# A hybrid trunk's S5 outputs with inputs and states as the stationary operand, and their way back to channels by TensorE

## The chip, the cores and the metric

The kernel runs on one core of a Trainium2 chip. The metric is the device time of one execution in microseconds (us). Five engines work beside each other, each through its own instructions in order: TensorE (PE), VectorE (DVE), ScalarE (ACT), GpSimd (POOL) and SyncE (SP), which issues most DMA transfers.

## The reference, cut to what matters

A trunk of two layers works on 512 tokens, 256 of context and 256 latent, of 1024 channels. In each layer four token mixers of 256 channels each (gated linear attention, retention, S5 and a gated delta rule) stand beside each other, and then a mixture of experts follows. The change touches the S5 mixer alone: a complex diagonal state-space model in both directions in 16 groups of 16 channels with 64 states, then a gelu and a gate.

```python
    ug = uf.reshape(B_, T, S5_GROUPS, S5_GROUP_CH)
    bu = lax.complex(jnp.einsum('gpc,btgc->btgp', b_re.astype(F32), ug),
                     jnp.einsum('gpc,btgc->btgp', b_im.astype(F32), ug))
...
    h = _bidirectional(run_f, run_b, ctx_f, lat_f, ctx_b, lat_b, h0)
    cmat = lax.complex(c_re.astype(F32), c_im.astype(F32))
    y = jnp.real(jnp.einsum('gcp,btgp->btgc', cmat, h)).reshape(B_, T, MIX_W) + d_skip.astype(F32) * uf
    y = jax.nn.gelu(y)
    return y * jax.nn.sigmoid(y @ glu_w.astype(F32) + glu_b.astype(F32))
```

## The kernel before

Activations stand with channels on the 128 partitions and tokens along the free dimension. In `mixers()` a layer projects its normed input to all heads (`project()`, L1387), weight block by weight block: every product is three fp32r products (`product3`, of a high and a low part of the weights and of the input). These are by far the most of TensorE's instructions in this part of the program. Blocks of the conditioning products (`ps_mods`, L1300 and L1305) lie between them. Beside the projections run the delta rule `dn()` and S5 `s5()`. Later come the GLA, retention, the output projection and the experts.

S5 works on chunks of 8 tokens. A chunk's input of a group is a column of 128 values (8 steps by 16 channels), and there are 64 chunks. In layer 1 only the last 32 are needed for the output (c0 = 32; nch is 64 in layer 0 and 32 in layer 1). For each half of the groups (8 groups at a time) it makes matrices (`ps_s_kk`, then s_T through DRAM scratch, s_E, s_inj), brings the inputs into states (`ps_s_I`, L1107), copies them (s_I, L1110), combines and scans them (L1115 to L1127) into the chunk states s_W (L1130 to L1133), and makes the outputs: the matrix Tm (s_T) times the inputs u plus the matrices E times the states W, into one PSUM bank `ps_s_y` (L1142, L1144). Tm and E are stationary and the chunks move, so the outputs stand with (step, channel of a group) on the partitions and (group, chunk) along the free dimension. ScalarE copies them out (L1146). A gelu by s_z follows (L1148 to L1155). The gate wants channels on the partitions. So SP writes s_y to a DRAM scratch (L1156) and 16 DMAs bring it back as s_yt (L1164). The gate is the product `ps_s_glu` (L1171), a sigmoid and a multiplication (s_out, L1177), which the output projection reads as mix_hi.

The delta rule prepares its chunk matrices on VectorE: dn_kt (L661) and dn_x (L688) from TensorE's `ps_dn` products (L654, L685), a blocked inversion in dn_G, dn_X and dn_P (L474 to L497), a round trip of dn_G through DRAM to dn_bd (L704, L724), then the products with dn_bd and dn_x (L743) and the recursion over chunks (L776, L786 and later).

The order of the instructions on each engine is not the order of the code. A scheduler with a simulated timeline chooses among the ready instructions by priorities that the code gives (`k.order(...)` with a small table for each layer), within the PSUM banks and buffers of two tracks. S5's first part, its outputs and its gate are three steps of one generator, with priorities of their own.

Of the kernel before, what the change touches and what calls it, by code (L numbers as in the profile page):

```python
# [6 lines left out]
F32 = mybir.dt.float32  # L7
# [3 lines left out]
AF = mybir.ActivationFunctionType  # L11
ALU = mybir.AluOpType
# [967 lines left out]
def s5(k, dram, dramk, st, get, bc, dskip, gw, gb, t0):  # L980
# [3 lines left out]


    nc, C = k.nc, k.C
    v, e = nc.vector, nc.gpsimd
    lr, li, bsr, bsi, r8, c8, s8 = st
    c0 = 32 * (t0 // 2)
    nch = 64 - c0  # L990
    f, b = slice(0, 64), slice(64, 128)
# [91 lines left out]
    for n in (1, 2, 4, 8, 16, 32):  # L1083
        m = min(n, 63 - n)
# [5 lines left out]
    su = get()  # L1090
    d0 = dram[0].rearrange("(s c) (h g n) -> h s g c n", s=8, h=2, g=8)
    for h in range(2):
        for s in range(8):
            nc.sync.dma_start(d0[h, s], su[:, h, s])
    u = k.u("s5_u")
    nc.sync.dma_start(u, dram[0])
    u = u.rearrange("p (g n) -> p g n", g=16)
    y = None
    for h in range(2):
# [36 lines left out]
        if y is None:  # L1136
            y = k.u("s5_y", 16 * nch).rearrange("p (g n) -> p g n", g=16)
        p = k.bank("s5_y")
        pv = p[:, :8 * nch].rearrange("p (g n) -> p g n", g=8)
        for g in range(8):  # L1140
            gg = 8 * h + g
            nc.tensor.matmul(pv[:, g], Tm[:, g], u[:, gg, c0:], start=True, stop=False)  # L1142
            for i in range(2):
                nc.tensor.matmul(pv[:, g], E[i][:, g].rearrange("p t c -> p (t c)"), W[i][:, gg, c0:], start=False,  # L1144
                                 stop=i == 1)
        nc.scalar.activation(y[:, hs], pv, AF.Copy)  # L1146
    z = k.u("s5_z", 16 * nch).rearrange("p (g n) -> p g n", g=16)
    nc.scalar.activation(z, y, AF.Square)  # L1148
# [5 lines left out]
    sigmoid(nc, z)  # L1154
    e.tensor_tensor(y, y, z, ALU.mult)  # L1155
    nc.sync.dma_start(dram[1][:, :16 * nch], y)  # L1156
    yield
    k.track = "b"

    d1 = dram[1][:, :16 * nch].rearrange("(s c) (h g n) -> h s g c n", s=8, h=2, g=8)  # L1160
    yt = k.u("s5_yt", 16 * nch).rearrange("p (h s n) -> p h s n", h=2, s=8)
    for h in range(2):
        for s in range(8):
            nc.sync.dma_start(yt[:, h, s], d1[h, s])  # L1164
    gw = gw()
# [41 lines left out]


def small_params(a):


    def per_part(x):

        x = np.asarray(x)
        return np.moveaxis(x.reshape(-1, 128), 1, 0)
# [20 lines left out]
    for i in range(2):  # L1236
# [5 lines left out]
        blocks[f"skip{i}"] = d.reshape(128, 64)  # L1242
        blocks[f"glu_b{i}"] = per_part(np.asarray(a["s5_glu_b"])[i])
        dl = np.asarray(a["ret_decay_logit"])[i]
# [12 lines left out]
def arrays(a):  # L1257
# [9 lines left out]
    for j, load in enumerate(LOADS):  # L1267
        cols = np.concatenate([w[..., SECTIONS[n][0]:SECTIONS[n][1]] for n in load], -1)
        out[f"w_in{j}"] = cols.transpose(0, 2, 1, 3).reshape(2, 128, -1)
    out["w_out"] = a["w_out"].reshape(2, 8, 128, 4, 256).transpose(0, 3, 2, 1, 4).reshape(8, 128, 2048)  # L1270

# [9 lines left out]
    bc = []  # L1281
# [4 lines left out]
    out["s5_bc"] = np.stack(bc, 2).reshape(2, 128, 1024)  # L1286
    out["glu_w"] = a["s5_glu_w"].reshape(2, 2, 128, 256).transpose(0, 2, 1, 3).reshape(2, 128, 512)
    return {n: np.ascontiguousarray(x, dtype=np.float32) for n, x in out.items()}
# [154 lines left out]
def mixers(k, I, P, S, modulated, load_w, between, layer, bc):  # L1443
# [73 lines left out]
    if bc is None:  # L1517
        bc = k.u("s5_bc")
        nc.sync.dma_start(bc, I["s5_bc"][layer])
    m_s5 = s5(k, S["dram"][2:4], S["dram5"], S["s5"][layer], s5_in, bc.rearrange("p (a n) -> p a n", a=4),  # L1520
              P[f"skip{layer}"].rearrange("p (s c) -> p s c", s=4), glu_w, P[f"glu_b{layer}"], t0)
# [600 lines left out]
def trunk(tc, I, out):  # L2122
    nc = tc.nc
    from contextlib import ExitStack
    with ExitStack() as st:
# [20 lines left out]
        def rows(src):  # L2146
            x = Rows(k, "xT", T, "b")
            for i, t in enumerate(x.t):
# [6 lines left out]
        mod = [pp.tile([128, 48, 2], F32, name=f"mod{i}") for i in range(2)]  # L2155
        S = dict(dram=[dr.tile([128, 1024], F32, name=f"scratch{i}") for i in range(4)],
                 dram5=[dr.tile([16, 8, 240], F32, name=f"scratch5{i}") for i in range(2)],
# [111 lines left out]
```

## Time and profile before

| | us |
|---|---|
| median of 3 runs | 1472.41 (1470.89 to 1476.87) |
| the profiled execution | 1470.13 |
| its span, first to last instruction | 1468.2 |
| TensorE busy | 1304.2 |
| VectorE busy | 786.3 |
| ScalarE busy | 467.1 |
| mean granted clock of TensorE | 0.937 |

Layer 0's mixers with their output projection run to about 470 us, and its experts follow. The projections of layer 1 begin at 847, its output projection ends at about 1180, and its experts end the program. The profile is of one execution. Times in its rows count from the first instruction.

### The profile page before, as it was taken

To read this page: it belongs to the slowest core of one execution; us is meant where nothing else is said; L and a number is where in the kernel's file an instruction comes from. 1 tells how busy PE (TensorE), PEld (TensorE's weight loads), DVE (VectorE), ACT (ScalarE), POOL (GpSimd) and SP (SyncE) were. 2 spreads that over 40 slices of the span, in tenths; PEclk is the share of its full clock that TensorE was granted. 3 is DMA by queue.
4 is the path that set the end of the run, shared out by engine and by line. 5 is a ranking of instruction groups with operands and counts; after the bars stand their busy time and mean duration, and the time that the engine had idled before them with its cause. 6 is when DMAs were issued, how large, how long until landed. Compare 5 with 4: busy or idle time off the path is not lost. (4 is left out here: it accounts for less than half of the span.)

```text
span 1468.2 us, 28484 instructions
## 1 busy us (share of the span) xinstructions
PE 1304.2 (89%) x11874; PEld 960.7 (65%) x11874; DVE 786.3 (54%) x1560; ACT 467.1 (32%) x778; POOL 187.6 (13%) x265
## 2 busy tenths in 40 slices
PE   4899789999989799999897698968999969999996
PEld 2696569788765577667654396747877746555553
DVE  7799593557453645425524979496467640111112
ACT  4435213434343244323423524312434421000001
POOL 0004112346110000000002100111344100000000
PEclk8999878999999789999999897977999979999999
DMA  9333253245434459999999421254445736999994
GB/s 377 119 108 104 48 187 114 99 156 191 160 123 182 168 206 379 393 373 392 379 391 362 155 82 58 61 187 139 163 158 211 274 141 255 416 415 416 414 413 165
DMA packets 90783, 335.31 MB, mean 228 GB/s; under 512 B 33190, under 2 KB 38120, under 8 KB 62104
## 3 DMA queue, kind: packets, MB, share of 16 engines
q1 hardware_dynamic: 86696, 320.37, 57.6%
q0 software_dynamic: 1648, 7.54, 1.4%
q10 hardware_dynamic: 2304, 5.51, 1.0%
q8 instruction: 97, 1.59, 0.4%
q14 instruction: 38, 0.31, 0.1%
HBM read 312.96 MB, written 20.41 MB: 227 GB/s over the span
## 5 line engine op out<-in xcount | busy, mean ns | idle before, releaser
L1906 PE MATMUL ps_up<-w_moe,xe 128*64 128x256 f32 x1664 | 202.7, 386 | 2.0 <-PEq L1782 2.0
L1906 PEld LDWEIGHTS ps_up<-w_moe,xe 128*64 128x64 f32 x1664 | 122.0, 138 | 73.0 <-issue 20.2
L1387 PE MATMUL ps_project<-h_hi,wi_lo 128*128 128x256 f32 (+1 forms) x568 | 136.1, 306 | 13.0 <-DVE wi_lo L155 13.0
L1387 PE MATMUL ps_project<-h_hi,wi_hi 128*128 128x256 f32 (+1 forms) x568 | 136.8, 308 | 7.6 <-ACT h_hi L1375 4.0
L1387 PE MATMUL ps_project<-h_lo,wi_hi 128*128 128x256 f32 (+1 forms) x568 | 132.4, 300 | 0.3 <-DVE h_lo L1376 0.3
L1387 PEld LDWEIGHTS ps_project<-h_hi,wi_lo 128*128 128x128 f32 (+1 forms) x568 | 97.9, 203 | 20.9 <-DVE wi_lo L155 14.0
L1387 PEld LDWEIGHTS ps_project<-h_hi,wi_hi 128*128 128x128 f32 (+1 forms) x568 | 97.8, 203 | 12.1 <-ACT h_hi L1375 4.1
L1945 PE MATMUL ps_down<-w_moe,actT 128*64 128x512 f32 x416 | 98.2, 597 | 2.7 <-ACT actT L1929 2.7
L155 DVE TENSOR_TENSOR w_moe_lo<-w_moe,w_moe_hi 128x1024 fp32r<-128x1024 f32 x72 | 85.1, 1218 | 28.5 <-ACT w_moe_hi L154 28.5
L1387 PEld LDWEIGHTS ps_project<-h_lo,wi_hi 128*128 128x128 f32 (+1 forms) x568 | 97.3, 202 | 3.1 <-issue 0.9
L154 ACT ACTIVATE w_moe_hi<-w_moe 128x1024 fp32r<-128x1024 f32 x72 | 73.0, 1053 | 28.5 <-DMA w_moe<-in_w_moe 21.6
L1946 DVE COPY y<-ps_down 128x512 f32<-128x512 f32 x26 | 18.0, 691 | 109.4 <-PE ps_down L1945 109.4
L155 DVE TENSOR_TENSOR wi_lo<-ring,wi_hi 128x1024 fp32r<-128x1024 f32 (+1 forms) x50 | 61.0, 1222 | 23.9 <-ACT wi_hi L154 20.8
L154 ACT ACTIVATE wi_hi<-ring 128x1024 fp32r<-128x1024 f32 (+1 forms) x50 | 51.5, 1032 | 66.1 <-PE ps_project L1387 42.4
L1945 PEld LDWEIGHTS ps_down<-w_moe,actT 128*64 128x64 f32 x416 | 29.5, 137 | 51.5 <-issue 45.4
L1929 ACT ACTIVATE actT<-ps_actT 128x256 f32<-128x256 f32 x26 | 10.0, 383 | 154.0 <-PE ps_actT L1926 151.4
L1923 DVE TENSOR_TENSOR act<-act,ps_up 128x256 f32<-128x256 f32 (+1 forms) x32 | 14.9, 466 | 78.2 <-ACT act L1922 67.4
L1300 PE MATMUL ps_mods<-ring,sc 128*32 128x512 f32 x368 | 51.9, 649 | 3.5 <-DVE mod L1307 3.5
L1870 PE MATMUL ps_gather<-sel,h_hi 128*128 128x256 f32 (+1 forms) x256 | 49.6, 310 | 6.0 <-DVE sel L1977 4.0
L2143 POOL DMA_DIRECT2D ring<-in_w_in x4 | 2.5, 612 | 401.5 <-PE ps_up L1906 373.2
L1970 DVE COPY backT<-ps_back 128x256 f32<-128x256 f32 (+1 forms) x17 | 7.5, 439 | 86.4 <-PE ps_back L1968 81.5
L1870 PE MATMUL ps_gather<-sel,h_lo 128*128 128x256 f32 (+1 forms) x256 | 47.8, 303 | 0.0
(559 smaller groups left out, 2793.4 us busy)
## 6 DMA issues: line engine op xcount, KB each, us to landing
w_moe<-in_w_moe SPq DMA_DIRECT2D x144, 1024.0 KB
w_moe<-in_w_moe SPq DMA_DIRECT2D x96, 512.0 KB
ring<-in_w_ada SPq DMA_DIRECT2D x46, 1024.0 KB
ring<-in_w_in SPq DMA_DIRECT2D x21, 1024.0 KB
ring<-in_w_out SPq DMA_DIRECT2D x8, 1024.0 KB
xT<-in_xT SPq DMA_DIRECT2D x8, 512.0 KB
Y<-y ACTq DMA_DIRECT2D x6, 512.0 KB
ring<-in_w_in POOLq DMA_DIRECT2D x3, 1024.0 KB, 7.8
```

The lines of the kernel that those rows point to most:

```text
L154: self.nc.scalar.activation(out[0], src, AF.Copy)
L155: self.nc.vector.tensor_tensor(out[1], src, out[0].bitcast(F32), ALU.subtract)
L1300: nc.tensor.matmul(p[32 * j:32 * j + 32], sc[:, 4 * r + j], w[r][j], start=r == 0, stop=r == 1)
L1387: nc.tensor.matmul(p[:, c], x[a], w[b][:, c], start=i + a + b + o == 0, stop=i == n - 1 and a == 1, skip_group_check=True)
L1870: nc.tensor.matmul(p[:, i * n:(i + 1) * n], rows[:, ms], sel[j % nt], start=j == 0, stop=j == 2 * nt - 1)
L1906: nc.tensor.matmul(out[j][64 * c:64 * c + 64], x(4 * half + i), w(i)[:, 256 * c:256 * c + 256], **kw)
L1923: nc.vector.tensor_tensor(act, act, pu, ALU.mult)
L1929: nc.scalar.activation(aT, p[:, :n], AF.Copy)
L1945: nc.tensor.matmul(p[64 * half:64 * half + 64], aT[i], ds[half](i), start=i == 0, stop=i == 3)
L1946: nc.vector.tensor_copy(y, p)
L1970: nc.vector.tensor_copy(b, p[:, :nt * 128])
L2143: queue.dma_start(w[:, :n], src)
```

## The change

The operands of the output products trade places: a chunk column of u or W (128 by nch) is stationary and Tm or E (128 columns) moves. The outputs of a group then stand with chunks on the partitions (nch of them, at row nch*j of the array's columns) and (step, channel) along the free dimension; 128/nch groups (2 in layer 0, 4 in layer 1) lie beside each other on the partitions of one 128-column block. The gelu works on this form. Its last multiplication by GpSimd writes a new tile s_yp with groups of a step next to each other, and TensorE multiplies blocks of it (stationary) by the identity, which puts channels back on the partitions: 8 products of 128 by 128 in layer 0 and 16 of 64 by 64 in layer 1 (`ps_s_yt`), copied out by ScalarE in two copies or one. The channels then come in another order within the mixer (`s5_channels`), and the rows of the gate's weights and bias and of the output projection's weights are put into that order on the host. The write to DRAM, the 16 reads and the fourth scratch are gone.

```diff
@@ s5()
-    d0 = dram[0].rearrange("(s c) (h g n) -> h s g c n", s=8, h=2, g=8)
+    d0 = dram.rearrange("(s c) (h g n) -> h s g c n", s=8, h=2, g=8)
...
+    per = 128 // nch
+    ns = 8 // per
...
         if y is None:
-            y = k.u("s5_y", 16 * nch).rearrange("p (g n) -> p g n", g=16)
-        p = k.bank("s5_y")
-        pv = p[:, :8 * nch].rearrange("p (g n) -> p g n", g=8)
-        for g in range(8):
-            gg = 8 * h + g
-            nc.tensor.matmul(pv[:, g], Tm[:, g], u[:, gg, c0:], start=True, stop=False)
-            for i in range(2):
-                nc.tensor.matmul(pv[:, g], E[i][:, g].rearrange("p t c -> p (t c)"), W[i][:, gg, c0:], start=False,
-                                 stop=i == 1)
-        nc.scalar.activation(y[:, hs], pv, AF.Copy)
-    z = k.u("s5_z", 16 * nch).rearrange("p (g n) -> p g n", g=16)
+            y = k.u("s5_y", 16 * nch)
+        p = k.bank("s5_y")[:, :128 * ns]
+        for q in range(ns):
+            for i in range(3):
+                for j in range(per):
+                    g = per * q + j
+                    l = (W[i - 1] if i else u)[:, 8 * h + g, c0:]
+                    r = E[i - 1][:, g].rearrange("p t c -> p (t c)") if i else Tm[:, g]
+                    nc.tensor.matmul(p[nch * j:nch * j + nch, 128 * q:128 * q + 128], l, r, start=i == 0, stop=i == 2)
+        nc.scalar.activation(y[:, 128 * ns * h:128 * ns * (h + 1)], p, AF.Copy)
+    z = k.u("s5_z", 16 * nch)
...
-    e.tensor_tensor(y, y, z, ALU.mult)
-    nc.sync.dma_start(dram[1][:, :16 * nch], y)
+    yp = k.u("s5_yp", 16 * nch)
+    e.tensor_tensor(yp.rearrange("p (t b c) -> p b t c", t=8, c=16), y.rearrange("p (b t c) -> p b t c", t=8, c=16),
+                    z.rearrange("p (b t c) -> p b t c", t=8, c=16), ALU.mult)
     yield
     k.track = "b"

-    d1 = dram[1][:, :16 * nch].rearrange("(s c) (h g n) -> h s g c n", s=8, h=2, g=8)
-    yt = k.u("s5_yt", 16 * nch).rearrange("p (h s n) -> p h s n", h=2, s=8)
-    for h in range(2):
-        for s in range(8):
-            nc.sync.dma_start(yt[:, h, s], d1[h, s])
+    yt = k.u("s5_yt", 16 * nch).rearrange("p (a s n) -> p a s n", a=2, s=8)
+    m = 256 // per
+    for i in range(2 * nch // 64):
+        p = k.bank("s5_yt")
+        for j in range(512 // (2 * nch)):
+            t = 512 // (2 * nch) * i + j
+            for x in range(per // 2):
+                nc.tensor.matmul(p[m * x:m * x + m, 2 * nch * j:2 * nch * (j + 1)], yp[:, t * m:(t + 1) * m],
+                                 C["ident"][:, 2 * nch * x:2 * nch * (x + 1)], start=True, stop=True)
+        ts = slice(512 // (2 * nch) * i, 512 // (2 * nch) * (i + 1))
+        nc.scalar.activation(yt[:, :, ts], p.rearrange("p (s a n) -> p a s n", a=2, n=nch), AF.Copy)
...
+def s5_channels(layer):
+
+    a, p = np.arange(256) // 128, np.arange(128)[None].repeat(2, 0).reshape(-1)
+    if layer:
+        g = 4 * (p % 64 // 16) + 2 * (p // 64) + a
+    else:
+        g = 2 * (p // 16) + a
+    return 16 * g + p % 16
```

The numbers of lines after it are higher, by 1 to 11 within `s5()` and by 24 from `project()` on (L1387 becomes L1411).

The scheduler's order changes beyond the edited lines. On VectorE in layer 0, this is where the delta rule's dn_kt, dn_x and dn_G stand before (s_kk belongs to S5's matrices, s_I and s_t to its second half):

```order
L621 SCALAR_TENSOR_TENSOR dn_t_2475<-dn_ab,consts_76,dn_t_2475 128x4x4 x2
L661 TENSOR_TENSOR dn_kt<-ps_dn,dn_dec 128x8x32 x8
L671 STREAM_TRANSPOSE dn_x<-dn_kt 128x512
L688 TENSOR_TENSOR dn_x<-ps_dn,dn_t_2475 128x8x32 x2
L1063 TENSOR_TENSOR s_kk<-s_kk,params 16x2x16 x3
...
L720 MEMSET dn_bd 128x2048
L1110 COPY s_I<-ps_s_I 64x512
L487 TENSOR_REDUCE dn_X<-dn_P 128x128
L1110 COPY s_I<-ps_s_I 64x512
...
L1116 TENSOR_TENSOR s_t<-s_W,s_I 128x512
```

And now (s_W is the last step of S5's second half):

```order
L621 SCALAR_TENSOR_TENSOR dn_t_2474<-dn_ab,consts_76,dn_t_2474 128x4x4 x2
L1114 COPY s_I<-ps_s_I 64x512
L1119 TENSOR_TENSOR s_t<-s_W,s_I 128x512
...
L1129 TENSOR_TENSOR s_I<-s_W,s_t 128x512
L661 TENSOR_TENSOR dn_kt<-ps_dn,dn_dec 128x8x32 x4
L1131 TENSOR_TENSOR s_t<-s_W,s_t 128x512
L1130 TENSOR_TENSOR s_t<-s_W,s_t 128x512
L661 TENSOR_TENSOR dn_kt<-ps_dn,dn_dec 128x8x32 x4
L671 STREAM_TRANSPOSE dn_x<-dn_kt 128x512
L1134 TENSOR_TENSOR s_W<-s_t,s_I 64x8x63
...
L1137 TENSOR_TENSOR s_W<-s_t,s_I 64x8
L688 TENSOR_TENSOR dn_x<-ps_dn,dn_t_2474 128x8x32 x2
...
L474 TENSOR_SCALAR dn_G<-dn_N 128x16
```

S5's copies, its combination, its scan (L1126) and its states s_W moved ahead of the second part of dn_kt, of dn_x and of dn_G.

On TensorE in layer 0, before, from the end of S5's second half of outputs to the first products of the delta rule with dn_bd, and further to the S5 gate (here and below most of the projections between are left out):

```order
L1142 MATMUL ps_s_y<-s_u,s_T 128x64
L1144 MATMUL ps_s_y<-s_W,s_E 128x64 x2
L1387 MATMUL ps_project<-h_hi,wi_lo 128x256 x2
...
L1387 MATMUL ps_project<-h_hi,wi_hi 128x256
L743 MATMUL ps_dn<-dn_bd,dn_x 32x32 x2
L1387 MATMUL ps_project<-h_hi,wi_hi 128x256
...
L743 MATMUL ps_dn<-dn_bd,dn_x 32x32 x62
L1387 MATMUL ps_project<-h_hi,wi_lo 128x256 x2
...
L1171 MATMUL ps_s_glu<-s_yt,glu_w 128x512 x4
...
L186 MATMUL ps_gla<-gla_zg 128x256 x4
```

And now (ps_s_yt are the products with the identity):

```order
L1149 MATMUL ps_s_y<-s_T,s_u 64x128 x2
L1149 MATMUL ps_s_y<-s_E,s_W 64x128 x4
L1411 MATMUL ps_project<-h_hi,wi_hi 128x256 x2
...
L1172 MATMUL ps_s_yt<-consts_75,s_yp 128x128 x8
L1411 MATMUL ps_project<-h_hi,wi_hi 128x256 x2
...
L1182 MATMUL ps_s_glu<-s_yt,glu_w 128x512 x4
...
L186 MATMUL ps_gla<-gla_zg 128x256 x4
...
L198 MATMUL ps_gla<-consts_76,gla_la 128x128 x2
L743 MATMUL ps_dn<-dn_bd,dn_x 32x32 x2
L1411 MATMUL ps_project<-h_hi,wi_hi 128x256 x2
...
L743 MATMUL ps_dn<-dn_bd,dn_x 32x32 x62
```

The outputs of S5's second half, its gate and the first GLA products stand ahead of the products with dn_bd, which before stood ahead of the gate. Of the 1176 projection products of layer 0, 652 stood ahead of S5's second half of outputs and 700 ahead of the 62 products with dn_bd; now these are 552 and 772. In layer 1 the 62 products stood after 1824 projection products, counted from the start, and stand after 1848.

## Rows read from the trace of the kernel before

**Rows 1.** The page: busy us, share of the span and instructions of TensorE.

```profile
PE 1304.2 (89%) x11874; PEld 960.7 (65%) x11874; DVE 786.3 (54%) x1560; ACT 467.1 (32%) x778; POOL 187.6 (13%) x265
```

**Rows 2.** Busy time of each engine (instructions), TensorE clock, DMA share, GB/s, by stretch.

```profile
140.00:240.00 100.00, 81.55 (x1122) 68.09 (x1120) 70.47 (x137) 21.65 (x38) 15.86 (x14) 0.81 0.39 125
180.00:200.00 20.00, 15.98 (x84) 12.51 (x85) 19.88 (x24) 2.25 (x3) 0.00 (x0) 0.66 0.49 184
260.00:280.00 20.00, 20.00 (x301) 16.29 (x297) 13.44 (x34) 10.14 (x21) 6.26 (x11) 1.00 0.12 44
```

**Rows 3.** Timeline of TensorE, a wait and the products with dn_bd and dn_x.

```profile
180.71 0.69 PE L1142 MATMUL ps_s_y<-s_u,s_T 128*128 128x64 f32 x2 [6.68 <-DVE s_I L1110]
...
231.66 1.25 PE L743 MATMUL ps_dn<-dn_bd,dn_x 32*32 32x32 f32 x124
```

**Rows 4.** Timeline of TensorE (start, us, instruction), S5 outputs of layer 0; evictions by tile.

```profile
107.06 0.56 PE L1144 MATMUL ps_s_y<-s_W,s_E 128*128 128x64 f32 x4
...
112.11 0.42 PE L1387 MATMUL ps_project<-h_hi,wi_hi 128*48 128x512 f32 x1
...
213.90 0.83 PE L1144 MATMUL ps_s_y<-s_W,s_E 128*128 128x64 f32 x4 [1.58 <-DVE s_W L1133]
...
223.45 0.78 PE L1387 MATMUL ps_project<-h_hi,wi_lo 128*128 128x256 f32 x2
...
L1146 ACT ACTIVATE s_y<-ps_s_y x4: 366/490/601, 112.9 to 1008.9; 128x512 f32<-128x512 f32 x2, 128x256 f32<-128x256 f32 x2
```

**Rows 5.** Timeline of TensorE, products of the delta rule in layer 0.

```profile
240.93 1.09 PE L776 MATMUL ps_dn<-dn_bd,dn_ke 128*64 128x128 f32 x16
241.96 1.55 PE L786 MATMUL ps_dn<-dn_VB,dn_bd 128*128 128x64 f32 x12
243.44 1.09 PE L776 MATMUL ps_dn<-dn_bd,dn_ke 128*64 128x128 f32 x16
```

**Rows 6.** Timeline of TensorE, products that the new order moves, layer 0.

```profile
208.62 1.92 PE L1300 MATMUL ps_mods<-ring,sc 128*32 128x512 f32 x16
...
262.88 3.70 PE L1171 MATMUL ps_s_glu<-s_yt,glu_w 128*128 128x512 f32 x8
...
270.93 1.99 PE L186 MATMUL ps_gla<-gla_zg 33*128 33x256 f32 x8
...
277.74 2.05 PE L198 MATMUL ps_gla<-consts,gla_la 128*128 128x128 f32 x16
...
284.61 1.05 PE L1305 MATMUL ps_mods<-consts,mods 128*128 128x2 f32 x8
...
371.70 0.40 PE L1387 MATMUL ps_project<-h_hi,wi_hi 128*128 128x256 f32 x2
371.94 0.40 PE L1387 MATMUL ps_project<-h_lo,wi_hi 128*128 128x256 f32 x2
```

**Rows 7.** Timelines of the SyncE queue and of ScalarE, S5 in layer 0.

```profile
240.66 9.99 SPq L1164 DMA_DIRECT2D s_yt<-scratch  x16
...
373.40 1.06 ACT L154 ACTIVATE mix_hi<-s_out 128x1024 fp32r<-128x1024 f32 x1 [1.10 <-PE ps_project L1387]
```

**Rows 8.** Timeline of VectorE, layer 0, delta rule and S5; in brackets idle time before.

```profile
153.09 1.42 DVE L661 TENSOR_TENSOR dn_kt<-ps_dn,dn_dec 128x256 f32<-128x256 f32 x4 [6.53 <-PE ps_dn L654]
...
166.51 0.18 DVE L474 TENSOR_SCALAR dn_G<-dn_N 128x16 f32<-128x16 f32 x1 [2.04 <-DMA scratch<-s_kk]
...
179.96 0.69 DVE L1110 COPY s_I<-ps_s_I 64x512 f32<-64x512 f32 x1
...
213.59 0.17 DVE L1133 TENSOR_TENSOR s_W<-s_t,s_I 64x8 f32<-64x8 f32 x1
...
216.23 1.23 DVE L769 TENSOR_TENSOR dn_ke<-dn_rows,dn_eg 128x1024 f32<-128x1024 f32 x1
225.44 0.69 DVE L1149 TENSOR_SCALAR s_z<-s_z 128x1024 f32<-128x1024 f32 x1 [7.98 <-ACT s_z L1148]
```

**Rows 9.** Waits of TensorE between 850 and 1180 us: total, times, longest.

```profile
PE ps_s_y L1144 <- DVE s_W L1133: 6.0, 1, 6.0
```

More of the change, by code (lines that the diff above doesn't have):

```diff
@@ L1095, in s5 @@
     u = k.u("s5_u")
-    nc.sync.dma_start(u, dram[0])
+    nc.sync.dma_start(u, dram)
     u = u.rearrange("p (g n) -> p g n", g=16)
+    per = 128 // nch
+    ns = 8 // per
     y = None
@@ L1242, in small_params @@
         blocks[f"skip{i}"] = d.reshape(128, 64)
-        blocks[f"glu_b{i}"] = per_part(np.asarray(a["s5_glu_b"])[i])
+        blocks[f"glu_b{i}"] = per_part(np.asarray(a["s5_glu_b"])[i][s5_channels(i)])
         dl = np.asarray(a["ret_decay_logit"])[i]
@@ L1269, in arrays @@
         out[f"w_in{j}"] = cols.transpose(0, 2, 1, 3).reshape(2, 128, -1)
-    out["w_out"] = a["w_out"].reshape(2, 8, 128, 4, 256).transpose(0, 3, 2, 1, 4).reshape(8, 128, 2048)
+    ch = [s5_channels(i) for i in range(2)]
+    w = np.stack([np.concatenate([x[:512], x[512:768][ch[i]], x[768:]]) for i, x in enumerate(a["w_out"])])
+    out["w_out"] = w.reshape(2, 8, 128, 4, 256).transpose(0, 3, 2, 1, 4).reshape(8, 128, 2048)
     g = a["moe_w_gate"].reshape(32, 2, 4, 128, 512).transpose(0, 1, 3, 2, 4).reshape(32, 2, 128, 2048)
@@ L1286, in arrays @@
     out["s5_bc"] = np.stack(bc, 2).reshape(2, 128, 1024)
-    out["glu_w"] = a["s5_glu_w"].reshape(2, 2, 128, 256).transpose(0, 2, 1, 3).reshape(2, 128, 512)
+    w = np.stack([x[ch[i]][:, ch[i]] for i, x in enumerate(a["s5_glu_w"])])
+    out["glu_w"] = w.reshape(2, 2, 128, 256).transpose(0, 2, 1, 3).reshape(2, 128, 512)
     return {n: np.ascontiguousarray(x, dtype=np.float32) for n, x in out.items()}
@@ L1519, in mixers @@
         nc.sync.dma_start(bc, I["s5_bc"][layer])
-    m_s5 = s5(k, S["dram"][2:4], S["dram5"], S["s5"][layer], s5_in, bc.rearrange("p (a n) -> p a n", a=4),
+    m_s5 = s5(k, S["dram"][2], S["dram5"], S["s5"][layer], s5_in, bc.rearrange("p (a n) -> p a n", a=4),
               P[f"skip{layer}"].rearrange("p (s c) -> p s c", s=4), glu_w, P[f"glu_b{layer}"], t0)
@@ L2155, in trunk @@
         mod = [pp.tile([128, 48, 2], F32, name=f"mod{i}") for i in range(2)]
-        S = dict(dram=[dr.tile([128, 1024], F32, name=f"scratch{i}") for i in range(4)],
+        S = dict(dram=[dr.tile([128, 1024], F32, name=f"scratch{i}") for i in range(3)],
                  dram5=[dr.tile([16, 8, 240], F32, name=f"scratch5{i}") for i in range(2)],
```

## The prediction

> **What bounds the kernel now.** I read the page first, for the share of TensorE, then the times by stretch, then the timeline of TensorE and VectorE in the mixers of layer 0, then the SyncE queue and the waits. TensorE is busy 89% of the span [rows 1], but that is a mean. In the mixers of layer 0 two kinds of stretch follow each other [rows 2]: from 140 to 240 us TensorE is busy 81.55 of 100 us at a mean granted clock of 0.81 (0.66 between 180 and 200), while from 260 on it is busy all the time at full clock. In the first, VectorE sets the pace (19.88 of 20 us between 180 and 200): it prepares the delta-rule block (dn_kt, dn_x, dn_G) and, in between, the second half of the S5 scan. In the second, the sum of TensorE's work sets the pace, so what a step of TensorE is worth there is its full duration, and before 231.66, where the delta-rule products begin in earnest [rows 3], it is worth only what delays that point. The end of the mixer is then: the time at which those products begin, plus the TensorE work that is left behind them. I work with that.
>
> **The change part by part.**
>
> *The output products.* Layer 0 has 2 x 48 of them (in the trace every fp32 product is two records). The first half runs from 107.06 to 112.11, 5.05 us or 0.105 each; the second from 213.90 to 223.45, 9.55 us or 0.199 each, at a lowered clock [rows 4]. The new form, stationary 128x64 and 128 columns moving into two column halves in turn, has a neighbour in the trace: 16 records of 128*64 by 128x128 from 240.93 to 241.96 are 0.064 each, while the old form beside it takes 0.123 (12 in 1.48 us, the start of the next) [rows 5]. So 96 x 0.064 = 6.1 us in place of 14.6. For layer 1 (stationary 128x32, four column tiles) there is no row of that size; the bounds are 0.03 (a quarter of the mods product, 0.12 for 512 columns on four tiles [rows 6]) and 0.064. I take 0.04, 3.8 us for 96 in place of some 10.7 (96 at the 0.105 to 0.12 of the same old forms). Added are the products back to channels: 16 records of 128x128 in layer 0, at 0.12, 1.9 us; 32 of 64x64 in layer 1, at most 0.064, 2.0 us. The evictions of the results by ScalarE cost 0.37 to 0.60 us each [rows 4], three more in all; ScalarE idles in these stretches, but S5 waits for them. All of this lies ahead of the delta-rule products in layer 0, in the stretch where TensorE has slack, so by itself it is worth nearly nothing there.
>
> Between 240.93 and 243.44 the trace changes between the whole array and half of its columns twice [rows 5], and the 28 records in it are no further apart than in longer runs of either form, so a change costs 0.1 us at most, and the some 20 changes that the new products bring cost at most 2, in the slack again. The Trainium skill (TensorEngine Tiling (Array Packing), Key Properties) says that changing the tiling mode drains TensorE, and the new products use two modes; no drain of a size that counts is seen in this row, and the page gives no figure for one.
>
> *The round trip through DRAM.* One write and 16 reads of SyncE (9.99 us from 240.66) are removed in each layer [rows 7]. Its result is first wanted by the mixing at 373.4 [rows 7], 110 us after the products that read it begin at 262.88 [rows 6]. It is hidden, and I cost it at nothing; if the cover were gone, it would cost its 10 us and the write ahead of it, some 13. What it does move is the queue behind it: the loads of glu_w and of the ring start 13 us sooner, but TensorE does not wait for a load there.
>
> *The order.* This is the larger part. The order before and the order after are alike up to the first half of the products. Then (the extracts in the section on the change) the second half of S5 moves ahead. On VectorE its copies, scan and combination stand before the second part of dn_kt, dn_x and dn_G; before, they lay among the dn_P products behind dn_G. On TensorE, 72 more project products, one more block of mods, the S5 gate products, the GLA log-decay and its cumulative sum stand before the delta-rule products. Worked out: 72 x 0.12 (two start in the 0.24 us from 371.70 to 371.94) = 8.6; mods 1.92 + 1.05 = 3.0; gate 3.7; gla_zg 2.0; gla_la 2.05 [rows 6]. Together 19.3 us leave the stretch in which every us counts. They go into the stretch from 140 to 231, which has 18.5 us of TensorE idle between 140 and 240, and whose clock loses some 15 us more against full speed (81.55 busy times the missing 0.19) [rows 2]. The space, 33 to 34 us, holds them, less some 8 saved on the products, plus 1.9 for the way back: about 13 us.
>
> What it costs is the delay of the delta-rule block. Before, VectorE idles 6.53 us until 153.09, then goes to dn_G at 166.51 and to dn_ke at 216.23 [rows 8]; some 13.3 us of these 49.7 are the S5 operations (20 between those at 179.96 and 213.59, of 0.17 to 1.22 us each, their overlaps taken off). Put ahead they delay dn_G by 13.3 at most, less the idle time they fill. The block is then 49.7 - 13.3 = 36.4 us long, plus the S5 gelu and gate that now fall into it: seven operations between 0.69 (the one at 225.44) and 1.23 (the size of dn_ke), at 0.9 each 6.4. Nothing absorbed: 166.5 + 13.3 + 42.8 = 222.6, a delay of 6.4. All absorbed: 7 us earlier. Against it, the products for S5's matrices now stand before those of the delta rule on TensorE, and dn_x waits on TensorE behind the first S5 products, hence behind s_T's load. I take a delay of 9, from 4 to 16, nearest the row that absorbs nothing. A wait of 6.68 us at 180.71 (the bank of s_I) [rows 3] goes, since s_I is copied out early; but TensorE now reaches the S5 products sooner than s_W, which it waited 1.6 us for before: a wait of up to 10 us with the project products queued behind it, inside the slack. Gain of layer 0: 19.3 - 9 = 10.3.
>
> In layer 1 the same move is smaller: 24 project products (2.9) and one block of mods (3.0) come before the delta-rule products, 5.9 us against a delay of about 5, as S5 stays inside the dn_G block there. The wait of 6.0 us on s_W [rows 9] may shorten or not. I take +0.9, from -4 to +4.
>
> Sum against the profiled execution, 1470.1 us (span 1468.2 and 2 us around it; the median is 2.3 us above): 1470.1 - 10.3 - 0.9 = 1458.9; after layer 0 the order is unchanged, so a shift of the mixer passes on through the experts, whose loads start from the same queue. I forecast 1459.
>
> **The rivals.**
> *Given back.* The order puts work into the slack, but TensorE stands at s_y until s_W is there, the clock stays at 0.66 to 0.8 until the delta-rule products begin, and they begin at 231.66 + 16 or so. Then layer 0 gains 3 us and layer 1 nothing: 1467. For it speaks that a pause was followed by low clock before (the 6.68 us at 180.71 [rows 3], then 0.66 [rows 2]). Against it, that more work is ready in the stretch.
>
> *The delta rule becomes the bound.* VectorE works in order, and S5's chain from s_I to s_W now stands before dn_kt. If the first copy of s_I comes late, everything of the delta rule does. With the 13.3 us in full, the 6.5 us of dn_kt's old wait and 10 us for s_T and the products behind it, the delay is about 30: 1470.1 + 30 - 19.3 - 0.9 = 1480. It decides from a delay of 20 on, and the measured time is slower by over 0.5% from 28 on (the price of the moved work, 20.2, and 7.4). For it: VectorE had nothing else to do in the 6.53 us before dn_kt, and in the new order it has. Against it: dn_kt's operands are ready when S5's are.
>
> *More than forecast.* VectorE's idle time before dn_kt (6.5) and before dn_G (2.04 by itself) [rows 8] absorbs most of the S5 work, the delay is 0, and layer 1 gains 4: 1470.1 - 19.3 - 4 = 1447.
>
> *The form doesn't pack.* If column tiles of one bank do not run beside each other, the products take 0.105 to 0.12 as before: 5 us more in layer 0 and 7 in layer 1, half of it in slack. On the forecast this gives 1465. The Trainium skill (TensorEngine Tiling (Array Packing), Performance Considerations) holds the swap with two or four column tiles worth 2 and 4 times. The 0.064 against 0.123 [rows 5] agrees for two; no row here shows four.
>
> **How the numbers follow.** Half a per cent is about 7.4 us, and is what a measurement of this kernel can tell from no change. Forecast (1453 to 1463) 0.47, more than forecast 0.10, given back 0.23, doesn't pack 0.06, delta rule the bound 0.14. Faster by over 0.5% means under 1465: the forecast, more, and a part of the not-packed: 0.58. Within: given back and half of the not-packed, plus the mild end of the delta-rule case: 0.31. Slower: 0.11. The range for 8 in 10 is from 1447 to 1474: it leaves out most of the delta-rule case and the far side of the gain.
>
> **What would show it.** Right: in the trace after, dn_ke at 220 to 232 rather than 216, the delta-rule products at about 240, TensorE then full at clock 1.00 and the out projection 8 to 12 us earlier than before; the S5 records at 0.064 and 0.03 to 0.06. Wrong: the delta-rule products at 250 or later; TensorE with gaps among them; the 140 to 240 stretch still at 0.7 clock; or gains that disappear before the experts begin.

## The result and the profile after

The changed kernel takes 1480.49 us (median of 13 runs, 1475.77 to 1484.92), the kernel before 1472.41: a ratio of 1.0051, with a 95% interval from 1.0035 to 1.0066. The forecast was 1459, so the change is 0.5% slower where 0.9% faster was expected. The profiled execution of after took 1476.16 us (span 1474.3, against 1468.2); it is one of the fastest of the 13.

The first line of the page of after:

```profile
PE 1300.8 (88%) x11922; PEld 950.0 (64%) x11922; DVE 794.8 (54%) x1560; ACT 467.8 (32%) x781; POOL 185.7 (13%) x265
```

TensorE's busy time falls by 3.4 us (1304.2 before, [rows 1]) and the span grows by 6.1, so the time has gone into TensorE's idle time. Busy time by stretch, as in [rows 2], first of after, with the two stretches that the layer's mixers fall into at the end:

```profile
140.00:240.00 100.00, 84.58 (x996) 66.94 (x992) 79.02 (x144) 36.94 (x61) 18.37 (x17) 0.93 0.50 163
180.00:200.00 20.00, 18.22 (x142) 15.18 (x138) 18.45 (x43) 8.79 (x12) 7.59 (x4) 1.00 0.54 191
85.00:240.00 155.00, 135.30 (x1393) 110.34 (x1392) 132.27 (x220) 60.79 (x97) 22.63 (x21) 0.94 0.40 133
240.00:400.00 160.00, 147.99 (x2513) 128.17 (x2511) 89.84 (x178) 51.35 (x91) 65.58 (x98) 0.95 0.28 104
```

And the last two of before:

```profile
85.00:240.00 155.00, 134.58 (x1528) 113.54 (x1526) 124.55 (x214) 50.91 (x80) 27.38 (x19) 0.88 0.34 107
240.00:400.00 160.00, 156.06 (x2378) 131.46 (x2378) 87.33 (x182) 61.39 (x107) 65.57 (x99) 1.00 0.41 148
```

Busy time multiplied by the granted clock gives the work done, in us at full clock. From 140 to 240 it rises from 66.1 (81.55 x 0.81) to 78.7 (84.58 x 0.93): the slack took 12.6 us of work, about the 13 that the prediction put there. (From 85 to 240 it is 8.8 us, 134.58 x 0.88 to 135.30 x 0.94: the new order does less ahead of 140.) From 240 to 400 it falls from 156.1 to 140.6 (147.99 x 0.95), by 15.5. That stretch was full before; now it has 12.0 us of idle time in place of 3.9, and loses 7.4 us to the clock (147.99 x 0.05). Where the idle time is, the waits of TensorE between 240 and 400 in after tell (us in total, times, longest):

```profile
PE ps_gla L286 <- DVE gla_AD L298: 4.8, 2, 4.0
PE ps_gla L218 <- issue: 3.3, 1, 3.3
PE ps_project L1411 <- DVE wi_lo L155: 1.4, 1, 1.4
PE ps_gla L286 <- ACT gla_A L293: 1.1, 2, 0.7
```

The first four rows are shown. The same view of before, whole:

```profile
PE ps_dn L810 <- ACT dn_u L787: 2.3, 1, 2.3
PE ps_project L1387 <- DVE wi_lo L155: 1.7, 2, 0.9
```

TensorE's timeline in after shows the two longest of them, and what follows the first (start, us, instruction; in brackets the idle time before):

```profile
240.12 1.25 PE L743 MATMUL ps_dn<-dn_bd,dn_x 32*32 32x32 f32 x124
...
245.93 0.33 PE L218 MATMUL ps_gla<-consts,gla_ko 128*128 128x128 f32 x1
249.55 0.58 PE L218 MATMUL ps_gla<-consts,gla_ko 128*128 128x128 f32 x2 [3.29 <-issue]
249.93 0.42 PE L1329 MATMUL ps_mods<-consts,mods 128*128 128x2 f32 x2
250.21 0.77 PE L1411 MATMUL ps_project<-h_hi,wi_hi 128*128 128x256 f32 x2
250.79 0.63 PE L1411 MATMUL ps_project<-h_lo,wi_hi 128*128 128x256 f32 x2
251.21 0.63 PE L1411 MATMUL ps_project<-h_hi,wi_lo 128*128 128x256 f32 x2
...
255.98 1.97 PE L776 MATMUL ps_dn<-dn_bd,dn_ke 128*64 128x128 f32 x32
...
349.68 0.38 PE L286 MATMUL ps_gla<-gla_x 32*32 32x32 f32 x20 [3.96 <-DVE gla_AD L298]
```

The products with dn_bd begin at 240.12, 8.5 us later than before [rows 3], as forecast (9). But the recursion's first product (L776), at 240.93 before [rows 5], stands at 255.98, 15 us later. GLA's products with gla_ko have come forward, TensorE stands for 3.29 us in the middle of them, and the projections behind run at the 1.2 GHz level: two start in 0.42 us, against 0.24 us for two in [rows 6].

This wait is not one for data. All three products read gla_ko and write one bank. The first of them ran at 245.93, and the last write of gla_ko, on VectorE, had ended by then:

```profile
243.05 1.22 DVE L211 TENSOR_TENSOR gla_ko<-gla_ko,k_gqk 128x1024 f32<-128x1024 f32 x1 [0.94 <-ACT gla_ko L210]
```

"Issue" in such a row means that the profile shows nothing that was waited for. What the trace has just ahead is a packet of 16 KB on the DMA queue for instructions, landed at 248.16, 1.4 us before TensorE goes on. This is no accident of one place: over the 17 traces of this case, 64 of the 69 waits of TensorE above 0.5 us with no releaser end 1.2 to 1.7 us after such a packet has landed (a few of 8 KB), against 74 of the 1394 with a releaser. So TensorE most likely stood for its own instructions. No run here tests that. The wait of 3.96 us at 349.68 is one for data, for gla_AD from VectorE.

The products themselves are what was forecast. Layer 0, first half, then the products back to channels, then layer 1, in after:

```profile
110.39 0.61 PE L1149 MATMUL ps_s_y<-s_E,s_W 128*64 128x128 f32 x8
110.82 0.39 PE L1149 MATMUL ps_s_y<-s_T,s_u 128*64 128x128 f32 x4
111.04 0.61 PE L1149 MATMUL ps_s_y<-s_E,s_W 128*64 128x128 f32 x8
...
194.91 1.95 PE L1172 MATMUL ps_s_yt<-consts,s_yp 128*128 128x128 f32 x16
...
1000.98 0.65 PE L1149 MATMUL ps_s_y<-s_E,s_W 128*32 128x128 f32 x16 [0.36 <-DVE s_W L1137]
1001.44 0.40 PE L1149 MATMUL ps_s_y<-s_T,s_u 128*32 128x128 f32 x8
1001.66 0.62 PE L1149 MATMUL ps_s_y<-s_E,s_W 128*32 128x128 f32 x16
1002.25 0.50 PE L1411 MATMUL ps_project<-h_hi,wi_hi 128*128 128x256 f32 x2
...
1017.18 1.15 PE L1172 MATMUL ps_s_yt<-consts,s_yp 128*64 128x64 f32 x32 [1.25 <-POOL s_yp L1160]
```

Twelve records start in 0.65 us in layer 0 (110.39 to 111.04), 0.054 each, and 40 in 1.27 us in layer 1, 0.032 each, against 0.105 in the old form [rows 4].

### The profile page after: what moved, and what is told of

It is laid out like the page before. It is cut to its first block, busy times and chain, and to the rows that moved or that the text cites. A ratio compares the mean times of both kernels' runs of the same rounds, so it can differ in the third digit from the quotient of the medians.

```text
span 1474.3 us, 28522 instructions
## 1 busy us (share of the span) xinstructions
PE 1300.8 (88%) x11922; PEld 950.0 (64%) x11922; DVE 794.8 (54%) x1560; ACT 467.8 (32%) x781; POOL 185.7 (13%) x265
## 5 line engine op out<-in xcount | busy, mean ns | idle before, releaser
L1411 PE MATMUL ps_project<-h_hi,wi_lo 128*128 128x256 f32 (+1 forms) x568 | 135.8, 306 | 13.8 <-DVE wi_lo L155 13.8
L1411 PE MATMUL ps_project<-h_hi,wi_hi 128*128 128x256 f32 (+1 forms) x568 | 137.5, 310 | 11.9 <-ACT h_hi L1399 4.0
L1411 PE MATMUL ps_project<-h_lo,wi_hi 128*128 128x256 f32 (+1 forms) x568 | 134.0, 302 | 0.1
L1411 PEld LDWEIGHTS ps_project<-h_hi,wi_lo 128*128 128x128 f32 (+1 forms) x568 | 97.5, 202 | 25.0 <-DVE wi_lo L155 17.9
L1411 PEld LDWEIGHTS ps_project<-h_hi,wi_hi 128*128 128x128 f32 (+1 forms) x568 | 98.1, 204 | 18.4 <-ACT h_hi L1399 4.1
L1411 PEld LDWEIGHTS ps_project<-h_lo,wi_hi 128*128 128x128 f32 (+1 forms) x568 | 97.5, 202 | 3.7 <-issue 2.0
```

The lines of the kernel that those rows point to most:

```text
L1411: nc.tensor.matmul(p[:, c], x[a], w[b][:, c], start=i + a + b + o == 0, stop=i == n - 1 and a == 1, skip_group_check=True)
```

## The experiments

Three kinds of edit recur. A kernel *held* to an order is given dependences of issue order alone between neighbours on an engine, so that the scheduler has to put the same instructions into a given row; the work and the waits on data stay. A form is the old or the new one of the output products. A place in a layer is told as the time from that layer's first s_I product, which leaves out what came before. Ratios with their 95% intervals are to the kernel before on the same chip.

```diff
+        for e, stretches in STANDING.items():
+            for runs in stretches:
+                own = [rows[e][a + n] for a, m in runs for n in range(m)]
+                for a, b in zip(own, own[1:]):
+                    tc.add_manual_dep(b, a.name, mybir.DependencyInfo(mybir.DependencyClass.NoSync,
+                                                                      mybir.DependencyReason.DATA), reason="order")
```

Such times come from one profiled execution each, and executions of one order differ. The changed kernel and its repetition have the same order on every engine, and their layer 0 takes 330.4 and 336.4 us to the output projection. The two runs with a late gate share an order too, and their layer 1 takes 333.6 and 341.0 us to the gather of the experts. A difference of a few us between two single profiles therefore shows nothing by itself. For layer 0 there are four profiles with the changed kernel's order (the change, its repetition, the change in layer 0 alone, and the first of the last three runs): 330.4, 336.4, 330.5 and 330.2 us, with 10.5 to 12.1 us of idle time on TensorE from 240 to 400 and a clock of 0.91 to 0.96 there. With the order of before there are three (before, and the two runs with the change in layer 1 alone): 327.4, 324.7 and 326.4 us, with 1.7 to 3.9 us of idle time at 1.00.

**The form or the order.** The changed form, with TensorE, VectorE and ScalarE held to the order of before in both layers:

> The changed S5 (swapped operands, way back by TensorE), with TensorE, VectorE and ScalarE held to the order of the kernel before in both layers; the products with the identity stand just ahead of the gate. If the loss comes from the order alone, this is as fast as before or a little faster: 1465 to 1473 us, with the first delta-rule products (dn_bd, dn_x) at 228 to 232 us. If the loss comes from the new form itself (products, copies, drains), it stays: 1478 to 1483.

Measured 1491.94, a ratio of 1.0092 [1.0056, 1.0127], worse than the change itself, and outside both ranges. Neither theory holds as it stood.

The old form, with TensorE and most of VectorE held to the changed order:

> The S5 of before, round trip through DRAM and all, with TensorE held to the order of the changed kernel in both layers and VectorE too, save S5's and GLA's own operations. If the order is the cause: 1477 to 1488 (the order of the changed kernel, plus a gate that waits for the round trip, which in this order is no longer covered by work behind it). If the form is the cause: 1468 to 1474.

Measured 1534.56, 1.0396 [1.0362, 1.0430]. Its waits of TensorE between 85 and 400 us:

```profile
PE ps_s_y L1144 <- DVE s_W L1133: 20.5, 2, 13.2
PE ps_s_glu L1171 <- DMA glu_w<-in_glu_w: 11.9, 1, 11.9
```

The old form is slow to feed an early gate: the gate's weights queue behind the round trip of 17 transfers on SyncE, and TensorE stands 11.9 us (8.6 in layer 1). So the round trip cost nothing only as long as the gate stood late. The larger wait, 20.5 us on s_W (33.5 in layer 1), is not for anything that the form of the products makes: s_W comes from S5's own VectorE instructions, which were left free in this run, as was ScalarE. For that reason the run does not tell the form from the order.

The change in one layer alone, with the old form in the other (this one for layer 0, and the same with `layer == 1`):

```diff
+    new = layer == 0
+    m_s5 = (s5 if new else s5_old)(k, S["dram"][2] if new else S["dram"][2:4], ...
```

> The change in layer 0 alone, order left to the scheduler; layer 0's order is that of the changed kernel, layer 1's nearly that of before. If the whole loss sits in layer 0's moved work: 1478 to 1482. If the layers share it as the profiles suggest (3 us in layer 0, 1 to 3 in layer 1): 1474 to 1478.

> The change in layer 1 alone; layer 0 as before. If the whole loss sits in layer 0: 1470 to 1474. If layer 1 carries half: 1475 to 1478.

Layer 0 alone: 1478.64, 1.0024 [1.0003, 1.0046]. Layer 1 alone: 1471.16, 0.9985 [0.9958, 1.0012]. The two do not add up to 1.0051. The scheduler chooses another order for each; whether that is the reason is tested below.

**Is TensorE's work still the pace behind 240 us?** 72 projection products are repeated in layer 0 (nine behind each of eight first products, each overwriting the one ahead of it), 8.6 us of work, in a kernel held to its own order:

```diff
+            for _ in range(AGAIN[0] if i + a + b + o == 0 else 0):
+                m1 = nc.tensor.matmul(p[:, c], x[a], w[b][:, c], start=True, stop=False, skip_group_check=True)
...
+        AGAIN[0] = 9 if not layer and name in ("rv", "rg", "gg") else 0
```

> The changed kernel in its own order, with 72 projection products of layer 0's last three projections (rv, rg, gg) done again at the start of their sums: 8.6 us of TensorE work at full clock behind the delta-rule products, worth nothing. If, with the new order, the stretch from 240 to 410 us is no longer set by TensorE's sum (gaps, and half clock behind them), it costs 0 to 4 us. If TensorE's sum still sets that stretch, it costs 8.6.

> The kernel before in its own order with the same 72 products again. There TensorE is 98 to 100% busy at full clock from 260 to 400 us, so both theories expect the whole 8.6 us, at least 7: 1479 to 1486. If it costs less, the sum of TensorE's work did not set the end of that stretch before either, and the prediction's model was wrong from the start.

The stretch from 240 to 400 of the changed kernel with them:

```profile
240.00:400.00 160.00, 152.91 (x2489) 133.73 (x2475) 89.97 (x178) 50.42 (x88) 64.58 (x97) 0.97 0.27 99
```

And of the kernel before with them:

```profile
240.00:400.00 160.00, 160.00 (x2533) 138.02 (x2533) 88.05 (x184) 59.23 (x104) 65.06 (x98) 1.00 0.38 137
```

In the changed order layer 0's output projection begins 331.7 us after the first s_I product, against 330.4 without them (330.2 to 336.4 in the four profiles of that order): 8.6 us of work for at most 1.5 us. They fill idle time (7.1 us of it are left of 12.0) and the clock is 0.97. The two long waits, for gla_AD and in the gla_ko products, are still there, 3.8 and 2.9 us. Before, it goes from 327.4 to 333.6. By these single profiles TensorE's work is the pace of layer 0's mixers before and no longer after. The whole time does not bear this out: 1484.77 (1.0089 [1.0062, 1.0117]) is 0.38 points over the change, some 5.6 us, between the 0 to 4 and the 8.6 that were set against each other, and 1481.44 (1.0045 [1.0023, 1.0067]) is 0.45 points over before, no different within the intervals. Where the first loses what it was spared in layer 0 is not settled; its layer 1 took 5 us longer in the one profile of it, with a wait of 4.8 us that has no releaser.

**The place of the gate.** One number of layer 0's table gives the gate's step a later priority:

```diff
-    dict(early=0, esep=1, inv=0, conv=1, dn=0, front=0, s5a=1, s5b=1, s5c=1, gla=1, ...
+    dict(early=0, esep=1, inv=0, conv=1, dn=0, front=0, s5a=1, s5b=1, s5c=2, gla=1, ...
```

In the changed kernel, and there a second time on another chip, and in the kernel before:

> The changed kernel with one number of the scheduler's table changed: the gate of S5 (way back included) gets a later class in layer 0. TensorE then does 28 fewer projection products and the log-decay of GLA later than the delta-rule products. If the loss is work taken from the stretch that it covered, this returns part of it: 1468 to 1476. If the order is not the cause, it stays at 1478 to 1484.

> The changed kernel with the late gate once more, beside the others on one chip and with more rounds, since its gain (0.23% with an interval that touches none) is near what can be measured. Real: 0.996 to 0.999 of before. Luck: 1.000 to 1.004.

> The kernel before with the same one number changed as in the run with the late gate: S5's gate gets a later class in layer 0. Its S5 and its delta rule stand where they stood; only the gate and GLA's start move back (the gate from behind 751 to behind 792 projection products). If the late gate gained because of where the changed kernel's order puts the delta rule, the number alone does nothing here: 1470 to 1480. If the number is a gain by itself, 1460 to 1470.

In the changed kernel: 1469.34, 0.9977 [0.9954, 1.0001], and 1470.42, 0.9971 [0.9952, 0.9990]: faster than the change, and in the second run clear of before too. In the kernel before: 1488.19, 1.0083 [1.0060, 1.0107], slower than either range allowed, for a reason that was not looked into. The stretch from 240 to 400 of the first:

```profile
240.00:400.00 160.00, 156.91 (x2318) 131.78 (x2316) 86.47 (x179) 54.98 (x95) 69.35 (x97) 0.95 0.35 132
```

Its products with dn_bd begin at 232.66, a delay of 1 us instead of 8.5, behind 744 projection products instead of 772, and idle time in the stretch is 3.1 us. The output projection begins at 320.6 us, and at 321.8 in the repetition, some 6 us ahead of before (327.4): over half of the gain forecast for layer 0, but with the gate late. The new form allows this order and does not bring it.

The clock of this stretch is 0.95, as in the changed kernel, with a quarter of its idle time. Part of it is lost where TensorE had not waited at all:

```profile
285.00:302.00 17.00, 17.00 (x277) 14.71 (x274) 10.47 (x26) 6.64 (x13) 5.62 (x10) 0.99 0.36 133
302.00:312.00 10.00, 10.00 (x103) 8.35 (x102) 3.71 (x9) 0.00 (x0) 2.48 (x4) 0.50 0.38 141
```

So not all of the lost clock can be put down to waits.

**Do shorter products leave longer waits?** The kernel of the first experiment, with the output products done three times over (the first two results overwritten):

```diff
+            for again in range(3):
                 for i in range(3):
                     for j in range(per):
```

> The changed S5 in the old order as in the run held to it, with every output product done three times over (15.8 and 9.3 us at the measured rate, near the 14.6 and 10.7 of before). That run lost 14 us though TensorE had less to do. If it lost because shorter products leave TensorE waiting in longer pieces and the clock falls to 1.2 GHz behind them, more products give part of it back: 1478 to 1486. If it lost to the products' form or the way back, this one is slower still, 1495 or more. If neither, it stays at 1488 to 1494.

Measured 1496.13, 1.0162 [1.0126, 1.0198]: more work makes it slower, so the short products are not what hurts. The time lies in the range named for a loss to the form or the way back, but it does not show one: the added products are themselves work, 16.7 us at the measured rates, for 0.70 points (some 10 us). In the first experiment's kernel TensorE waits in layer 1 (1000 to 1090 us) for the blocks of the delta rule:

```profile
PE ps_dn L743 <- DVE dn_bd L729: 9.1, 1, 9.1
```

The tripled one waits 6.7 us there. Layer 1 takes 349.3 and 349.8 us to the gather of the experts in these two, against 334.5 before: the order of before, held, fits the new form badly in layer 1. Why it does was not taken apart.

**Layer 0's order by itself.** The changed form with the order of before held in layer 0's mixers, and layer 1 left to the scheduler; and the changed kernel with S5's second half given the first priority:

```diff
+        if h and not t0:
+            k.order(0)
```

> The changed S5 with the old order held in layer 0 alone; layer 1 is left to the scheduler. The run with the old order in both layers lost 14 to 15 us, by its profile 5 in layer 0 and the rest in layer 1. If that is so, this one takes 1476 to 1484. If the loss was of the new form in either layer, 1488 or more.

> The changed kernel with S5's second half in layer 0 put in the same class as the delta rule: its outputs come as early as in the changed kernel, the delta-rule products behind 744 instead of 772 projection products, the recursion's end behind 888 instead of 969, and the scheduler then also starts layer 1's delta rule 80 products earlier. If what counts is that the delta-rule recursion starts early, with projections left to cover it, this is as fast as with the late gate or faster: 1462 to 1472. If S5 ahead of the delta rule is itself the loss, 1478 to 1486.

The first took 1475.65, 1.0005 [0.9987, 1.0022]. Its stretch from 240 to 400 is full again, as before:

```profile
240.00:400.00 160.00, 157.06 (x2504) 133.59 (x2494) 88.19 (x184) 61.57 (x108) 65.41 (x98) 1.00 0.39 142
```

Yet its output projection begins after 330.7 us, like the change (330.4): by these two, the order that fills the slack and the one that keeps the stretch behind it full end layer 0 at the same time. The second took 1478.09, 1.0027 [1.0005, 1.0049], just inside the range named for S5 ahead of the delta rule being the loss. Its layer 0 does not show that loss: it is 6.6 us shorter than before (320.8, with 1.7 us of idle time on TensorE from 240 to 400). All of it and more is given back later: 4.2 us between layer 0's output projection and layer 1's first s_I product, and 4.0 in layer 1, whose order the scheduler had also chosen anew (338.5 us to the gather).

**Layer 1's order by itself.** Three kernels beside each other on one chip: the changed kernel with layer 1 held to the order that it has when only layer 1 is changed; the change in layer 1 alone with layer 1 held to the order of the changed kernel; the changed kernel again.

> The changed kernel with layer 0 held to its own order and layer 1 held to the order that the scheduler chose when only layer 1 was changed (GLA's first products and the recursion's end a few products later). The change in layer 0 alone lost 0.24%, in layer 1 alone gained 0.15% (not clear), in both lost 0.51%: if the difference is the order that the scheduler chose for layer 1, this is 1.000 to 1.003 of before. If it lies in layer 0, or the single results are off, 1.004 to 1.006.

> The change in layer 1 alone, with layer 1 held to the order it has in the changed kernel and layer 0 to that of before. If layer 1's order is what makes both layers together worse: 1.001 to 1.004 of before. If not: 0.996 to 1.000, as the change in layer 1 alone.

> The changed kernel once more, beside the two others on one chip, to compare them without another chip's offset: 1.0035 to 1.0066 of before, as measured.

They took 1472.31, 0.9994 [0.9977, 1.0011]; 1479.11, 1.0030 [1.0008, 1.0052]; and 1480.94, 1.0052 [1.0035, 1.0069]. The first and the last are the same kernel with the same order in layer 0; the order in layer 1 alone makes 8.6 us between the medians. The middle one against the change in layer 1 alone (0.9985) says the same from the other side: 0.45 points. The two orders differ little: S5's copies, scan and states stand a few places further back among the delta rule's inversion (dn_G, dn_X, dn_P) on VectorE in the slower one (48 of its operations ahead of the last s_W, against 44), and GLA's first products (L186) behind the first recursion products instead of ahead of them on TensorE. The time from the first s_I product to layer 1's output projection is 282.8, 284.1 and 284.5 us with the slower order (the change, its repetition, the middle kernel) and 278.9 and 281.1 with the faster (the first kernel, the change in layer 1 alone). From its first product to its last the output projection takes 28.8 us in each of the three, against 27.0 in both. Waits of TensorE from 1095 to 1192 in the repeated change:

```profile
PE ps_out_project L1411 <- DVE wo_lo L155: 2.7, 3, 1.4
PE ps_gla L286 <- DVE gla_AD L298: 1.7, 1, 1.7
```

And in the first of the three:

```profile
PE ps_gla L286 <- DVE gla_AD L298: 2.4, 1, 2.4
...
PE ps_out_project L1411 <- ACT mix_hi L154: 2.1, 1, 2.1
...
PE ps_out_project L1411 <- DVE wo_lo L155: 0.3, 1, 0.3
```

The 35 us ahead of the output projection by clock, first the repeated change (it begins at 1166.0), then the first kernel (at 1154.2):

```profile
1131.00:1166.00 35.00, 31.89 (x340) 23.77 (x340) 20.24 (x49) 7.43 (x14) 14.80 (x29) 0.76 0.59 215
```

```profile
1119.18:1154.18 35.00, 31.93 (x406) 23.01 (x405) 22.48 (x55) 10.17 (x18) 14.89 (x30) 0.85 0.65 240
```

In these 35 us TensorE runs at 0.76 of its clock in all three profiles of the slower order, and at 0.85 and 0.90 in the two of the faster (0.90 in before). Within the output projection the slower order waits 2.7 us for the low part of its weights (wo_lo) and 0.3 for mix_hi, the faster 0.3 and 2.1, so the waits there differ little. The kernel before has the same 2.7 us on wo_lo, so that wait is not the change's. One wait is in all three profiles of the slower order and in neither of the faster, and it is again one without a releaser (the row is of the change, then the times of all three):

```profile
PE ps_dn L751 <- issue: 2.6, 1, 2.6
```

It is 2.6, 2.4 and 2.7 us. That the order of layer 1 makes the difference is shown by the medians; where in the layer it does is read from single profiles. Which of the few exchanged places brings it was not taken apart further, and stays open.

## Why the prediction was wrong

**The cost of the products: right.** 0.054 and 0.032 us a record stand against 0.064 and 0.04 assumed, 1.95 and 1.15 us for the way back against 1.9 and at most 2.0, 0.60 us for a copy by ScalarE against 0.37 to 0.60. The Trainium skill (TensorEngine Tiling (Array Packing), Performance Considerations) names the swap with 2 and 4 times column tiling for a moving side of 64 and 32; 0.105 over 0.054 and 0.032 is 1.9 and 3.3 times here.

**The round trip at nothing: right as to the gain.** It was hidden, and no gain from its removal is seen in the time. The cover was smaller than the 110 us given for it: the reads' last instruction ended at 250.65 (240.66 and 9.99), and the gate's products, which read them, stood in TensorE's order at 262.88, 12 us later. That it would be in the way of an early gate (11.9 us in the old form with the new order) was not among the steps.

**The delay of the delta rule: right in size for its first products.** 8.5 us against 9, from 4 to 16; dn_ke at 225.94 within the 220 to 232 named; the wait for s_I's bank gone, the one for s_W 2.8 us. The recursion's first product is 15 us late, since the gla_ko products and the wait in them now stand ahead of it.

**The slack takes the work: right in the main.** 12.6 us more were done between 140 and 240, against about 13 (8.8 from 85 on). The clock there rose from 0.81 to 0.93.

**"Together 19.3 us leave the stretch in which every us counts": this step failed.** The prediction counted them at their full duration, as if the stretch behind stayed full without them. It was full before: 1.7 to 3.9 us of idle time in 160 us, and 72 products added there begin the output projection 6.3 us later for 8.6 us of work. Once the work has gone, it is not: in the profile of after the waits are 12.0 us and the granted clock falls to a mean of 0.95, and much the same holds in all four profiles with this order. Of the waits, 3.3 us lie in the gla_ko products and have no releaser, and 4.8 are for gla_AD from VectorE. With a late gate, where 28 projection products and GLA's start stand behind the delta-rule products again, both long ones are gone. 8.1 us of added idle time and 7.4 us of clock are 15.5 us; with the 8.5 us of delay they outweigh the 19.3 by 4.7 us, where the trace has the output projection 5.2 us later, or 3.0 counted from the first s_I product. The run with the change in layer 0 alone says 0.24% of loss (0.03 to 0.46), some 3.5 us. That the lost clock follows from the waits is not shown: with a late gate 3.1 us of waits go with 0.95 as well. The prediction had its own rival for gains given back, but put it ahead of 240, on s_W and the clock there, where neither came about. The rival that named 1480 is not borne out either: it needed a delay of about 30, and that its number was met is luck.

**Layer 1, "+0.9, from -4 to +4": mis-sized, and of the wrong sign.** The wait for s_W [rows 9] stayed, now in two parts (waits of TensorE from 850 to 1180 in after):

```profile
PE ps_s_y L1149 <- DVE s_W L1137: 6.0, 2, 5.7
```

Its products and the order's first part were read, its end was not. The changed kernel's order of layer 1 costs 0.30% with the change in that layer alone, some 4.4 us, and the order that the scheduler finds when layer 0 is left as it was has no loss (0.9985, an interval that holds 1). So about half of the 8 us of loss lies in layer 1's order, which the prediction did not work on, and about half in layer 0 (0.24 and 0.30 points, with intervals of some 0.2 either way, against 0.51 for the whole change). Against the forecast layer 0 is the larger miss: 3.5 us lost where 10.3 were to be gained, against 4.4 lost where it was 0.9. With the faster order in layer 1 the whole change is 0.9994 of before, neither a gain nor a loss.

**Sum.** Layer 0's gain of 10.3 us was a loss of some 3.5, and layer 1's 0.9 one of some 4.4. The range, 1447 to 1474, took both terms from one reading of the order. It had no width for an order that differs in a layer whose work hardly changed, which by these runs is worth about half a per cent.

## What to carry to other kernels

Work that is moved off a full stretch is worth its duration only if what stays behind is ready without it: list the short waits that the moved work covered, and ask what TensorE will do while they last. Where a scheduler sets the order, an edit changes the whole row behind it; hold the order to tell the edit from the order, in each layer apart, and look for the version that takes the good part of both (here one number for the gate's place, 0.9971 to 0.9977 of before). Read more than one profile of an order before a difference of a few us is explained: here two of one order differed by 6 us in layer 0. A transfer that is hidden is hidden by the present order, and its removal pays only if the order makes use of it.

## What the runs showed of the hardware

Column tiles of one bank run beside each other for fp32 products with a moving side of 128 columns: 0.032 us a record with four tiles of 32, 0.054 with two of 64, against 0.12 for a record of 128 columns on the whole array. In the rows shown, the last 16 records ahead of a whole-array product take 0.59 us to its start (1001.66 to 1002.25), and 16 of the same kind 0.46 (from 1000.98), so the change costs some 0.13 us at most.

An idle time of 3.29 us on TensorE up to 249.55 was followed by 4.9 us at the 1.2 GHz level. Waits are not the only thing that goes with that level: with the late gate TensorE fell to it for 10 us at 302 after 17 us in which it was busy all the time. And one order does not always get one clock: from 240 to 400 us it was 0.95 in the changed kernel and 0.91 in its repetition, with 12.0 and 12.1 us of idle time.

Waits of TensorE for which the profile shows no releaser end, in 64 of 69 cases, 1.2 to 1.7 us after a packet on the instruction queue has landed; here they were 3.29 us in layer 0 and 2.4 to 2.7 in layer 1.
